# A fixed TensorE order for the experts' stage, weight buffers cut from one tile by hand, and the last weights in three transfers

## The chip, the cores and the metric

The kernel runs on one core of one Trainium2 chip, and reads all its weights from device memory. The metric is the device time of one execution in microseconds (us), where less is better. Engines are named as the profile names them: PE is TensorE, DVE is VectorE, ACT is ScalarE, POOL is GpSimd, and SP is the queue from which nearly all weight transfers are issued.

## The reference

Two blocks are computed in float32 for 256 tokens of width 1024:

```
def first_block(x, ...):
    for l in range(2):
        x = layer_norm(ALPHA * x + swiglu_half(x, w1[l], w3[l], w2[l]), ...)   # d_ff 2816
        h = x @ w_in[l]
        ...      # spatial gating, gated delta rule, gated linear attention
        x = layer_norm(ALPHA * x + mix @ w_out[l], ...)
        x = layer_norm(ALPHA * x + swiglu_half(x, ...), ...)

def second_block(x, c, ...):
    ...          # modulation from c, two kinds of attention, residual
    h2 = rms_norm_2(x, norm2_g) * (1.0 + scale2) + shift2
    return x + gate2 * moe_ffn(h2, ...)

def moe_ffn(h, ...):                     # 32 experts, the 4 best of each token
    ...
    gu = xe @ w_gate_up[e] + b_gate_up[e]                 # 1024 -> 2048
    g = min(gu[:, :1024], 7); u = clip(gu[:, 1024:], -7, 7)
    act = (u + 1) * (g * sigmoid(1.702 * g))
    y = act @ w_down[e] + b_down[e]                       # 1024 -> 1024
    # y times the token's gate, summed over its four experts
```

Each expert has 12 MiB of weights, so the 32 experts read 402.65 MB.

## The kernel before

**Dense stages** (the first block and the second block's attention). Weights come in transfers of 1 MB (0.5 MB for the first four) into `raw`, a pool of two buffers of 2 MB. `raw_half` (L142) gives out the two halves of one buffer, one after the other, and takes the next buffer when both are gone; `piece` (L151, transfer on L154) fills a half. `split` (L186, L187) makes of each 128x1024 part a rounded `wh` on ACT and a remainder `wl` on DVE, which TensorE multiplies (L161 and others). A framework's scheduler sets the order in which instructions stand on each engine and puts in the waits; a new buffer of a pool waits until every reader of the old one is done. On ACT and DVE the splits stand in one row with the work on the products (`tmp` L295, `ab` L297, `sl` L299, `gT` L302).

**Experts' stage.** Every expert gets 64 slots for tokens, and a part after it, skipped here, repeats experts that have more. `moe_order` (L1140) lists the 192 pieces of 2 MB: four of `gate_up` for an expert, then two of `down` for the expert before it. `moe_slots` (L1165) names nine buffers in turn, two of them from `raw`, and `prefetch` (L1173, transfer on L1177) issues a piece as soon as the buffer's last reader is done. Per expert, TensorE does this:
- `gate_up` (L1220): four pieces of 16 records each (L1230: every float32 matmul shows as two) into a two-bank PSUM tile `gu`, then the bias as eight records of a 32-row product (L1234).
- DVE and ACT make `act` of `gu` (L1237 to L1241).
- `down` (L1244), for the expert before: four transposes of `act` into the first bank of a tile `td` (L1249), a copy to SBUF on ACT (`aT`, L1251), two pieces of 16 records into the second bank (L1256), the bias (L1259), the product with `g2` on DVE, which gives `y` (L1261); two transposes of the gates (L1264), their copy `GT` on ACT (L1266), and `y` back to the tokens' places in eight records (L1270) that add up in four further banks over all experts.
- Every fourth expert `tokens` (L1196) gathers the tokens of the next four, with 32 records (L1207) and two copies on ACT (L1208).

All PSUM tiles come from pools in turn, and the scheduler decides what stands between what; it puts transposes and gathers between pieces. `moe` (L1345) has the loop, and `leave` (L1282 to L1285) copies the sums out and writes the result.

Of the kernel before, what the change touches and what calls it, by code (L numbers as in the profile page):

```python
# [16 lines left out]
P = 128  # L17
D = 1024
KD = D // P
T = 256  # L20
# [17 lines left out]
class Kernel:  # L38
    def __init__(self, ctx, tc, a, out):
# [4 lines left out]
        self.raw = pool("raw", 2)  # L44
# [8 lines left out]
        self.uid, self.spare = 0, None  # L53
# [1086 lines left out]
    def moe_order(self):  # L1140

        for e in range(33):
            if e < 32:
                yield from (self.gu_piece(e, i) for i in range(4))
            if e:
                yield from (self.dn_piece(e - 1, q) for q in range(2))
# [18 lines left out]
    def moe_slots(self):  # L1165

        self.spare = None
        while True:
            for name in ("rawE", "xp", "slotp", "raw", "slotp", "raw", "raw2", "slotp", "raw2"):
                tag = {"xp": "xT", "slotp": "slot"}.get(name, name)  # L1170
                yield getattr(self, name).tile([P, 4096], F32, tag=tag, name=self.n("rawm"))

    def prefetch(self, n, queue=None):  # L1173
        for _ in range(n):
            src, r = next(self.order), next(self.slots)
            v = r.rearrange("p (k f) -> p k f", k=src.shape[1])
            (queue or self.nc.sync).dma_start(v, src)  # L1177
            self.ready.append(v)

    def moe_piece(self, src):  # L1180
        if src is not None:
            r = self.raw.tile([P, 4096], F32, tag="raw", name=self.n("rawm"))
            v = r.rearrange("p (k f) -> p k f", k=src.shape[1])
# [12 lines left out]
    def tokens(self, XT, lo, hi):  # L1196
# [3 lines left out]
        for k0 in range(0, KD, 4):  # L1200
            w = self.wide()
            wv = w.rearrange("p a (b c) -> p (a b) c", b=2)[:, :, lo:hi]
            for k in range(4):
                i, j = divmod(k0 + k, 2)
                for t in range(2):
                    h = self.h2[t].rearrange("p (i m j) -> p i j m", i=4, j=2)[:, i, j]
                    nc.tensor.matmul(wv[:, k], h, at[:, t, lo:hi], start=(t == 0), stop=(t == 1))  # L1207
            nc.scalar.activation(XT[:, k0 : k0 + 4, lo:hi], wv, AF.Copy)  # L1208
# [11 lines left out]
    def gate_up(self, src, sel, XT):  # L1220
        nc = self.nc
        gu = self.wide()
        for i in range(4):
            r = self.moe_piece(src(i))
            for j in range(2):
                k = 2 * i + j
                for b in range(2):
                    for c in range(2):
                        f0 = b * 1024 + c * 512
                        nc.tensor.matmul(gu[c * 64 : c * 64 + 64, b], XT[:, k], r[:, j, f0 : f0 + 512], start=(k == 0), stop=False)  # L1230
        for b in range(2):
            for c in range(2):
                j = slice(32 * (2 * b + c), 32 * (2 * b + c) + 32)
                nc.tensor.matmul(gu[c * 64 : c * 64 + 64, b], sel[j], self.bgu[j], start=False, stop=True)  # L1234
        g, u, s = self.mg, self.mu.pop(0), self.ms
        self.mu.append(u)
        nc.vector.tensor_scalar(g, gu[:, 0], 7.0, None, op0=OP.min)  # L1237
        nc.vector.tensor_scalar(u, gu[:, 1], 7.0, -7.0, op0=OP.min, op1=OP.max)
        nc.scalar.activation(s, g, AF.Sigmoid, scale=1.702)  # L1239
        nc.vector.scalar_tensor_tensor(u, u, 1.0, g, op0=OP.add, op1=OP.mult)  # L1240
        nc.vector.tensor_tensor(u, u, s, op=OP.mult)  # L1241
        return u

    def down(self, src, sel, act, G, acc, first, last):  # L1244
        nc = self.nc
        td = self.wide()
        av = act.rearrange("p (m s) -> p s m", s=4)
        for s in range(4):
            nc.tensor.transpose(td[:, 0, s * P : (s + 1) * P], av[:, s], self.ident)  # L1249
        aT = self.aT  # L1250
        nc.scalar.activation(aT, td[:, 0].rearrange("p (s c i) -> p s c i", s=4, c=2), AF.Copy)  # L1251
        for q in range(2):
            r = self.moe_piece(src(q))
            for s in range(4):
                for c in range(2):
                    nc.tensor.matmul(td[c * 64 : c * 64 + 64, 1], aT[:, s, q], r[:, s, c * 512 : (c + 1) * 512],  # L1256
                                     start=(q == 0 and s == 0), stop=False)
        for c in range(2):
            nc.tensor.matmul(td[c * 64 : c * 64 + 64, 1], sel[0:32], self.bd[:, c * 512 : (c + 1) * 512], start=False, stop=True)  # L1259
        y = self.ms  # L1260
        nc.vector.tensor_tensor(y, td[:, 1], self.g2, op=OP.mult)  # L1261
        tg = self.wide()
        for t in range(2):
            nc.tensor.transpose(tg[:, 0, t * P : (t + 1) * P], G[t].rearrange("p d s -> p (d s)"), self.ident)  # L1264
        GT = self.GT
        nc.scalar.activation(GT, tg[:, 0, :T], AF.Copy)  # L1266
        for t in range(2):
            for c in range(2):
                r = slice(c * 64, c * 64 + 64)
                nc.tensor.matmul(acc[t][c], GT[r, t * P : (t + 1) * P], y[r, :], start=first, stop=first or last, skip_group_check=True)  # L1270
# [16 lines left out]
    def overflow(self, acc):  # L1287
# [3 lines left out]
        with tc.If(most > 64):  # L1291
            with tc.For_i(0, 32, 1) as e:
                have = nc.values_load(self.cnt[0:1, bass.ds(e, 1)], min_val=0, max_val=T)

                def part(r):
# [8 lines left out]
                    self.tokens(XT, 0, 64)  # L1304
                    G = self.gated(oh, [gt[:, t] for t in range(2)], 1)
                    gu = lambda i: self.gu_piece(e, i)
                    dn = lambda q: self.dn_piece(e, q)
                    self.down(dn, sel, self.gate_up(gu, sel, XT[:, :, :64]), [g[:, 0] for g in G], acc, False, True)
# [378 lines left out]
```

## Time and profile before

| | us |
|---|---|
| median of three runs | 2303.39 (2297.19 to 2309.14) |
| profiled execution, own time | 2300.92 |
| its span | 2299.1 |
| PE busy in the span | 2167.1 (94%) |
| start of the experts' pieces on PE | 1352.57 |
| start of the last eight records (L1270) | 2289.36 |

The span is the profiled execution from the first to the last instruction; its own time is 1.82 us longer. PEclk is the TensorE clock granted, as a share of full speed.

### The profile page before, as it was taken

Reading aid. Unit: us, or ns where it says so; the run is one execution under the profiler, and the core shown is the slowest. Engines: PE = TensorE matmul, PEld = TensorE weight load, DVE = VectorE, ACT = ScalarE, POOL = GpSimd, SP = SyncE. Lnnn points to the kernel's source line nnn. Section 1 sums busy time; section 2 is a strip of 40 time slices with the busy share of each in tenths; the row PEclk is TensorE's granted clock in tenths of the full one; section 3 lists DMA queues with packets and bytes.
Section 4 is the critical chain, followed back from the end, with each engine's and each line's share of the span. In section 5 each row is a group of like instructions: output and inputs, shape, how many; then the busy total and the mean of one; then the engine's idle time right before and its main releaser. Section 6 shows DMA issues by size and latency. Waiting matters only on the chain. (4 is left out here: it accounts for less than half of the span.)

```text
span 2299.1 us, 27689 instructions
## 1 busy us (share of the span) xinstructions
PE 2167.1 (94%) x11342; PEld 1375.1 (60%) x11343; DVE 1063.3 (46%) x1656; ACT 752.8 (33%) x1110; POOL 187.9 (8%) x214
## 2 busy tenths in 40 slices
PE   7999998999899999899989789999999999999998
PEld 6888877888788887778867553333332333333332
DVE  5866866966776686676676721111111111101011
ACT  4555843555455584245547520000000000000000
POOL 1001222001100122200020300000000000000000
PEclk9999999999999999999999879999999999999999
DMA  8854432956775443266554379999999999999994
GB/s 255 311 184 155 142 105 86 326 188 200 266 256 183 151 138 116 73 218 217 177 210 153 123 295 420 412 425 425 427 427 428 428 427 427 428 428 428 427 427 182
DMA packets 193156, 637.63 MB, mean 277 GB/s; under 512 B 24128, under 2 KB 131616, under 8 KB 168448
## 3 DMA queue, kind: packets, MB, share of 16 engines
q1 hardware_dynamic: 175920, 622.95, 69.6%
q0 software_dynamic: 3760, 11.28, 1.7%
q10 hardware_dynamic: 13344, 1.57, 0.4%
q8 instruction: 91, 1.49, 0.3%
q14 instruction: 41, 0.34, 0.0%
HBM read 633.91 MB, written 1.86 MB: 277 GB/s over the span
## 5 line engine op out<-in xcount | busy, mean ns | idle before, releaser
L187 DVE TENSOR_TENSOR wl<-raw,wh 128x1024 fp32r<-128x1024 f32 x332 | 407.6, 1233 | 201.8 <-ACT wh L186 201.5
L186 ACT ACTIVATE wh<-raw 128x1024 fp32r<-128x1024 f32 (+1 forms) x350 | 366.5, 1051 | 375.7 <-PE w L161 136.1
L161 PE MATMUL w<-xT,wh 128*128 128x512 f32 x1344 | 478.1, 397 | 6.8 <-DVE ab L297 6.8
L1230 PE MATMUL w<-rawm,XT 128*64 128x512 f32 x2048 | 463.3, 599 | 2.1 <-ACT wh L1266 2.1
L162 PE MATMUL w<-xT,wl 128*128 128x256 f32 x1344 | 379.6, 282 | 0.0
L1230 PEld LDWEIGHTS w<-rawm,XT 128*64 128x64 f32 x2048 | 141.4, 137 | 279.0 <-issue 270.4
L1237 DVE TENSOR_SCALAR wl<-w 128x512 f32<-128x512 f32 x32 | 22.1, 692 | 608.9 <-PE w L1234 608.9
L161 PEld LDWEIGHTS w<-xT,wh 128*128 128x128 f32 x1344 | 254.9, 190 | 67.6 <-DVE ab L297 7.5
L162 PEld LDWEIGHTS w<-xT,wl 128*128 128x128 f32 x1344 | 254.1, 189 | 1.5
L1256 PE MATMUL w<-rawm,wh 128*64 128x512 f32 x1024 | 232.7, 598 | 3.7 <-ACT wh L1251 3.7
L309 PE MATMUL m<-wh,gT 128*128 128x512 f32 x592 | 190.9, 393 | 0.0
L1251 ACT ACTIVATE wh<-w 128x512 f32<-128x512 f32 x32 | 19.1, 597 | 449.2 <-PE w L1249 444.7
L1256 PEld LDWEIGHTS w<-rawm,wh 128*64 128x64 f32 x1024 | 68.2, 136 | 144.4 <-issue 139.7
L309 PEld LDWEIGHTS m<-wh,gT 128*128 128x128 f32 x592 | 111.2, 188 | 26.9 <-issue 1.7
L309 PE MATMUL m<-wl,gT 128*128 128x512 f32 x296 | 116.3, 393 | 0.0
L1261 DVE TENSOR_TENSOR wl<-w,wl 128x512 f32<-128x512 f32 x32 | 22.1, 692 | 191.5 <-PE w L1259 191.5
L386 PE MATMUL w<-wh,xT 128*128 128x512 f32 (+1 forms) x224 | 89.3, 399 | 6.0 <-DVE xT L236 6.0
L384 PE MATMUL w<-wh,xT 128*128 128x512 f32 (+1 forms) x224 | 90.7, 407 | 2.5 <-ACT pre L711 2.0
L385 PE MATMUL w<-wl,xT 128*128 128x512 f32 (+1 forms) x224 | 88.7, 396 | 4.5 <-DVE wl L187 4.5
L1216 POOL TENSOR_TENSOR G<-wl 128x256 f32<-128x256 f32 x32 | 19.7, 647 | 841.7 <-PE w L1264 825.7
L1239 ACT ACTIVATE wl<-wl 128x512 f32<-128x512 f32 x32 | 20.1, 629 | 207.5 <-DVE wl L1237 207.5
L1270 PE MATMUL m<-wl,wh 64*128 64x512 f32 x256 | 63.6, 613 | 18.6 <-DVE wl L1261 18.6
(469 smaller groups left out, 2740.6 us busy)
## 6 DMA issues: line engine op xcount, KB each, us to landing
rawm<-in_w_gate_up_dram SPq DMA_DIRECT2D x126, 2048.0 KB
raw<-in_ffn_w_dram SPq DMA_DIRECT2D x130, 1024.0 KB
rawm<-in_w_down_dram SPq DMA_DIRECT2D x64, 2048.0 KB
raw<-in_w_in_dram SPq DMA_DIRECT2D x36, 1024.0 KB
adaw<-in_w_ada_dram SPq DMA_DIRECT2D x48, 512.0 KB
raw<-in_w_out_dram SPq DMA_DIRECT2D x12, 1024.0 KB
rawm<-in_w_gate_up_dram POOLq DMA_DIRECT2D x2, 2048.0 KB, 8.5
raw<-in_w_in_dram SPq DMA_DIRECT2D x4, 544.0 KB
```

Of the source, the lines that this page charges most:

```text
L161: nc.tensor.matmul(w[:, ab], h[:, k], self.xT[:, k], start=(k == 0), stop=False)
L162: nc.tensor.matmul(w[:, ab, :T], l[:, k], self.xT[:, k, :T], start=False, stop=(k == KD - 1))
L186: nc.scalar.activation(h, v, AF.Copy)
L187: (low or nc.vector).tensor_tensor(l, v, h.bitcast(F32), op=OP.subtract)
L309: mm = lambda g, w, start, stop: nc.tensor.matmul(acc[t][q], g, w[:, 0, q * 512 : (q + 1) * 512], start=start, stop=stop, skip_group_check ...
L384: self.nc.tensor.matmul(w[:, t, :n], xh, h, start=(k == 0), stop=False)
L385: self.nc.tensor.matmul(w[:, t, :n], xh, l, start=False, stop=False)
L386: self.nc.tensor.matmul(w[:, t, :n], xl, h, start=False, stop=(k == KD - 1))
L1230: nc.tensor.matmul(gu[c * 64 : c * 64 + 64, b], XT[:, k], r[:, j, f0 : f0 + 512], start=(k == 0), stop=False)
L1237: nc.vector.tensor_scalar(g, gu[:, 0], 7.0, None, op0=OP.min)
L1256: nc.tensor.matmul(td[c * 64 : c * 64 + 64, 1], aT[:, s, q], r[:, s, c * 512 : (c + 1) * 512], start=(q == 0 and s == 0), stop=False)
L1270: nc.tensor.matmul(acc[t][c], GT[r, t * P : (t + 1) * P], y[r, :], start=first, stop=first or last, skip_group_check=True)
```

## The change

Four things change.
1. `raw` is one tile of four parts of 8 KB per partition, handed out by a counter (`raw_half`), and two neighbouring parts are one of the nine buffers of the experts (`raw_pair`). So the framework sees which part an instruction reads, and a load waits for the readers of its own part alone.
2. The experts' stage has two PSUM tiles, `gu` and `td`, for its whole length, and TensorE's instructions stand there in the order in which the code writes them (`manual_schedule`). The other engines are still ordered by the scheduler. The bias of each product comes first, and the gathered tokens go into `gu` and `td`.
3. The last expert's second `down` piece goes out as three transfers, of 1 MB, 0.5 MB and 0.5 MB, where other pieces are one.
4. `mu`, the buffer of `act`, is one where it was two in turn, and the sigmoid is issued before `u` is clipped.

```diff
-        self.raw = pool("raw", 2)
+        self.raw = pool("raw").tile([P, 4, 2048], F32, name="raw")
...
-        if self.spare is None:
-            x = self.raw.tile([P, 2, 2048], F32, tag="raw", name=self.n("raw"))
-            self.spare = x[:, 1]
-            return x[:, 0]
-        x, self.spare = self.spare, None
-        return x
+        return self.raw[:, next(self.turn) % 4]
+
+    def raw_pair(self):
+
+        i = 2 * (next(self.turn) % 2)
+        return self.raw[:, i : i + 2].rearrange("p k f -> p (k f)")
...
-                yield from (self.dn_piece(e - 1, q) for q in range(2))
+                yield from ((self.dn_piece(e - 1, q), (0, 2, 3, 4) if e == 32 and q else (0, 4)) for q in range(2))
...
-            (queue or self.nc.sync).dma_start(v, src)
+            for k0, k1 in itertools.pairwise(cuts):
+                (queue or self.nc.sync).dma_start(v[:, k0:k1], src[:, k0:k1])
...
+    def act_T(self, td):
+
+        av = self.mu.rearrange("p (m s) -> p s m", s=4)
         for s in range(4):
-            nc.tensor.transpose(td[:, 0, s * P : (s + 1) * P], av[:, s], self.ident)
...
+            self.nc.tensor.transpose(td[:, s * P : (s + 1) * P], av[:, s], self.ident)
+        self.nc.scalar.activation(self.aT, td.rearrange("p (s c i) -> p s c i", s=4, c=2), AF.Copy)
...
     def moe(self):
-        nc, a = self.nc, self.a
-        prev = G = None
+        with self.tc.manual_schedule(engines={mybir.EngineType.PE}):
+            acc = self.experts()
+        self.leave(acc)
+        self.overflow(acc)
+
+    def experts(self):
...
+        gu, td = self.wide(), self.wide()
+        XT, oh = self.gather(of(self.place, 0), 4)
+        for k0, w in ((0, gu), (4, td)):
+            self.tokens(XT, 0, 64, k0, w)
+        for e in range(34):
             if e < 32:
...
+                up = self.gate_up(gu, listed, sel(e), XT[:, :, (e % 4) * 64 : (e % 4) * 64 + 64])
+                next(up)
             if e == 0:
-                self.tokens(XT, 64, 256)
+                self.gates()
             if e == 1:
                 acc = [[self.bank() for _ in range(2)] for _ in range(2)]
...
+            if e > 1:
+                self.back(acc, e == 2, e == 33)
+            if e < 32:
+                next(up)
+            if 0 < e < 33:
+                self.gates_T(td[:, 0], [g[:, (e - 1) % 4] for g in G])
+            if e < 32:
+                drain(up)
...
+            if 0 < e < 33:
+                more = e % 4 == 3 and e < 31
+                dn = self.down(td[:, 1], listed, sel(e - 1))
...
+                for i, _ in enumerate(dn):
+                    if more and i in (1, 2):
+                        self.tokens(XT, 0, 256, 4 * i - 4, gu)
+            if e < 32:
+                self.act_T(td[:, 0])
+        return acc
```

Where the order moves can be seen at three places. The first is PE in the experts' stage before, from the `down` of one expert to the `gate_up` of the next (L1230, L1256: `gate_up` and `down` pieces; L1249: transposes of `act`; L1234, L1259: biases; L1264: transposes of the gates; L1270: back to the tokens):

```order
L1256 MATMUL w_13165<-rawm_13181,wh_11477 64x512 [waits DMAHW1_49]
L1256 MATMUL w_13165<-rawm_13181,wh_11477 64x512 x7
L1259 MATMUL w_13165<-wl_11479,eye_154 64x512 x2
L1270 MATMUL m_11744<-wl_11480,wh_11477 128x512 [waits DVE_49,Activation_49]
L1270 MATMUL m_11745<-wl_11480,wh_11477 128x512
L1270 MATMUL m_11746<-wl_11480,wh_11477 128x512
L1270 MATMUL m_11747<-wl_11480,wh_11477 128x512
L1230 MATMUL w_13208<-rawm_13209,XT_13094 64x512 [waits DMAHW2_49,PE_49]
L1230 MATMUL w_13208<-rawm_13209,XT_13094 64x512 x7
L1249 MATMUL w_13258<-ident,wh_11476 128x128 [waits PE_49]
L1249 MATMUL w_13258<-ident,wh_11476 128x128 x2
L1230 MATMUL w_13208<-rawm_13219,XT_13094 64x512 [waits DMAHW3_49]
```

After the change the same stretch is written on other lines (L1235, L1260: pieces; L1248: transposes of `act`; L1227, L1255: biases; L1270: transposes of the gates; L1279: back to the tokens; a wait is shown in square brackets):

```order
L1260 MATMUL w_11501<-rawm_12305,wh_11382 64x512 x7
L1248 MATMUL w_11501<-ident,wh_11381 128x128 [waits DVE_49]
L1248 MATMUL w_11501<-ident,wh_11381 128x128 x3
L1227 MATMUL w_11500<-wl_11383,eye_155 64x512 x4
L1235 MATMUL w_11500<-rawm_12325,XT_12186 64x512 [waits DMAHW2_49]
L1235 MATMUL w_11500<-rawm_12325,XT_12186 64x512 x7
L1279 MATMUL m_11623<-wl_11385,wh_11382 128x512
L1279 MATMUL m_11624<-wl_11385,wh_11382 128x512
L1279 MATMUL m_11625<-wl_11385,wh_11382 128x512
L1279 MATMUL m_11626<-wl_11385,wh_11382 128x512
L1235 MATMUL w_11500<-rawm_12339,XT_12186 64x512 [waits DMAHW3_49]
L1235 MATMUL w_11500<-rawm_12339,XT_12186 64x512 x7
```

The rows for the way back stood behind the bias of `down`; they now stand behind the first piece of the next expert but one, and the transposes of `act` stand in one place, directly behind the pieces of `down`, with a wait for DVE.

The second place is SP at the program's start before (`raw`: 1 MB of weights; `adaw`: modulation weights; `ln_g`, `ln_b`: a norm's two vectors, spread over the partitions):

```order
L154 DMA raw_192<-in_ffn_w_dram 128x8x128 x2
L154 DMA raw_195<-in_ffn_w_dram 128x8x128 x2
L767 DMA adaw_457<-in_w_ada_dram 128x1024
L767 DMA adaw_459<-in_w_ada_dram 128x1024
L191 DMA ln_g<-in_ln_g_dram 128x1024 [waits DMAHW0_49]
L191 DMA ln_b<-in_ln_b_dram 128x1024 [waits DMAHW1_49]
L154 DMA raw_343<-in_ffn_w_dram 128x8x256 [waits DMAHW2_49,DMAHW3_49,DVE_49,Activation_49]
L154 DMA raw_343<-in_ffn_w_dram 128x8x256
L154 DMA raw_485<-in_ffn_w_dram 128x2x1024 [waits DMAHW5_49,DMAHW4_49,DVE_49]
L154 DMA raw_485<-in_ffn_w_dram 128x8x256
```

After the change:

```order
L154 DMA raw<-in_ffn_w_dram 128x8x128 x4
L767 DMA adaw_455<-in_w_ada_dram 128x1024
L767 DMA adaw_457<-in_w_ada_dram 128x1024
L154 DMA raw<-in_ffn_w_dram 128x8x256 [waits DMAHW0_49,DMAHW2_49,DVE_49,Activation_49]
L154 DMA raw<-in_ffn_w_dram 128x8x256 [waits DMAHW1_49,DMAHW3_49,DVE_49,Activation_49]
L154 DMA raw<-in_ffn_w_dram 128x2x1024 [waits DMAHW4_49,DVE_49]
L154 DMA raw<-in_ffn_w_dram 128x8x256 [waits DMAHW5_49,DVE_49]
L191 DMA ln_g<-in_ln_g_dram 128x1024
```

The four loads of `raw` now stand ahead of `ln_g` and `ln_b`, and each has a wait of its own; before, the first of a pair waited for both old halves.

The third place is ACT at the same point before (`wh`: the split of a 128x1024 part, L186, the first two shown of the 0.5 MB loads; `tmp`: the first product leaves its PSUM tile, L295):

```order
L186 ACTIVATE wh_290<-raw_195 128x1024 [waits DMAHW4_49]
L186 ACTIVATE wh_310<-raw_195 128x1024 [waits DMAHW5_49]
L186 ACTIVATE wh_348<-raw_343 128x1024 [waits DVE_49,DMAHW2_49,PE_49,Activation_49]
L295 ACTIVATE tmp_279<-w_206 128x512 [waits PE_49]
L299 ACT_TABLE_LOAD
L299 ACTIVATE sl_283<-ab_281 128x256 [waits DVE_49]
```

After the change:

```order
L186 ACTIVATE wh_289<-raw 128x1024 [waits DMAHW4_49]
L186 ACTIVATE wh_309<-raw 128x1024 [waits DMAHW5_49]
L186 ACTIVATE wh_346<-raw 128x1024 [waits DVE_49,DMAHW0_49,PE_49,Activation_49]
L186 ACTIVATE wh_366<-raw 128x1024 [waits DVE_49,DMAHW1_49,PE_49,Activation_49]
L295 ACTIVATE tmp_278<-w_205 128x512 [waits PE_49]
L186 ACTIVATE wh_397<-raw 128x1024 [waits DVE_49,PE_49]
L299 ACT_TABLE_LOAD
L299 ACTIVATE sl_282<-ab_280 128x256 [waits DVE_49]
```

Behind the 0.5 MB parts, `tmp` now stands behind two splits, which read two different loads (each has a transfer of its own among its waits), where it stood behind one.

## Rows read from the trace of the kernel before

**Rows 1.** Windows of 57.5 us: busy time of each engine, PEclk, DMA share, GB/s

```profile
1782.50:1840.00 57.50, 56.97 (x264) 21.92 (x262) 6.50 (x10) 5.27 (x8) 1.68 (x3) 1.00 1.01 428
2242.50:2300.00 57.50, 45.69 (x207) 14.44 (x202) 6.29 (x10) 4.17 (x8) 0.00 (x0) 0.97 0.42 176
```

**Rows 2.** The chain that ended last, 1345 to 2299: shares, then start, us, line

```profile
by line: PE w L1230 48.0%; PE w L1256 24.0%; PE w L1207 6.9%; PE m L1270 6.6%; PE w L1259 3.4%; PE w L1234 3.4%; PE w L1249 2.7%; DVE wl L1261 1.5%; PE w L1264 1.3%; issue 0.5%; ACT wh L1266 0.5%; ACT wh L1251 0.3%; DVE xn L1284 0.1%; DVE w
...
1701.86 10.45 PE w L1230 x48
...
1818.66 10.45 PE w L1230 x48
```

**Rows 3.** The transfer queue's waits, 1200 to 2299: us in total, times, longest

```profile
SPq L1177 <- PE w L1230: 508.7, 106, 17.5
```

**Rows 4.** PE's timeline in the experts' stage: start, us, line, count, [idle <-releaser]

```profile
1814.50 4.16 PE L1207 MATMUL w<-wl,wh 128*128 128x256 f32 x18
...
1841.86 1.07 PE L1259 MATMUL w<-wl,eye 32*64 32x512 f32 x4
1843.82 1.99 PE L1270 MATMUL m<-wl,wh 64*128 64x512 f32 x8 [0.89 <-DVE wl L1261]
1845.74 3.65 PE L1230 MATMUL w<-rawm,XT 128*64 128x512 f32 x16
1849.32 0.63 PE L1249 MATMUL w<-ident,wh 128*128 128x128 f32 x3
1849.88 3.65 PE L1230 MATMUL w<-rawm,XT 128*64 128x512 f32 x16
1853.47 0.39 PE L1249 MATMUL w<-ident,wh 128*128 128x128 f32 x1
1853.78 7.09 PE L1230 MATMUL w<-rawm,XT 128*64 128x512 f32 x32
1860.80 1.09 PE L1234 MATMUL w<-wl,eye 32*64 32x512 f32 x8
1861.82 3.65 PE L1256 MATMUL w<-rawm,wh 128*64 128x512 f32 x16
1865.40 0.44 PE L1264 MATMUL w<-ident,G 128*128 128x128 f32 x2
...
1869.35 1.07 PE L1259 MATMUL w<-wl,eye 32*64 32x512 f32 x4
```

**Rows 5.** PE's timeline at the stage's start

```profile
1352.57 16.52 PE L1230 MATMUL w<-rawm,XT 128*64 128x512 f32 x64
...
1370.04 5.48 PE L1207 MATMUL w<-wl,wh 128*128 128x192 f32 x32
1375.45 13.95 PE L1230 MATMUL w<-rawm,XT 128*64 128x512 f32 x64
```

**Rows 6.** PE's timeline at the end

```profile
2289.36 1.99 PE L1270 MATMUL m<-wl,wh 64*128 64x512 f32 x8 [0.94 <-DVE wl L1261]
```

**Rows 7.** A window of 1 us near the last bytes

```profile
2266.00:2267.00 1.00, 1.00 (x10) 0.20 (x8) 0.00 (x0) 0.00 (x0) 0.00 (x0) 1.00 0.12 49
```

**Rows 8.** ACT's timeline in the first feed-forward part

```profile
32.82 1.06 ACT L186 ACTIVATE wh<-raw 128x1024 fp32r<-128x1024 f32 x1 [13.07 <-DMA raw<-in_ffn_w_dram]
33.78 0.58 ACT L295 ACTIVATE tmp<-w 128x512 f32<-128x512 f32 x1
```

**Rows 9.** The transfer queue's timeline at the start

```profile
20.00 9.50 SPq L154 DMA_DIRECT2D raw<-in_ffn_w_dram  x4
```

**Rows 10.** Windows of two stretches in the dense stages

```profile
30.00:36.00 6.00, 2.78 (x17) 2.20 (x16) 1.83 (x2) 3.06 (x4) 0.00 (x0) 1.00 1.07 373
36.00:42.00 6.00, 6.00 (x26) 5.16 (x26) 5.26 (x8) 5.23 (x9) 0.00 (x0) 0.72 0.59 210
580.00:590.00 10.00, 5.81 (x17) 3.97 (x16) 7.70 (x11) 3.68 (x5) 4.53 (x3) 0.66 0.71 217
```

**Rows 11.** ACT's timeline in the second layer

```profile
578.12 1.06 ACT L186 ACTIVATE wh<-raw 128x1024 fp32r<-128x1024 f32 x1 [4.10 <-DMA raw<-in_ffn_w_dram]
```

More of the change, by code (lines that the diff above doesn't have):

```diff
@@ L1143, in moe_order @@
             if e < 32:
-                yield from (self.gu_piece(e, i) for i in range(4))
+                yield from ((self.gu_piece(e, i), (0, 2)) for i in range(4))
             if e:
-                yield from (self.dn_piece(e - 1, q) for q in range(2))
+                yield from ((self.dn_piece(e - 1, q), (0, 2, 3, 4) if e == 32 and q else (0, 4)) for q in range(2))
     def gu_piece(self, e, i):
@@ L1181, in moe_piece @@
         if src is not None:
-            r = self.raw.tile([P, 4096], F32, tag="raw", name=self.n("rawm"))
-            v = r.rearrange("p (k f) -> p k f", k=src.shape[1])
+            v = self.raw_pair().rearrange("p (k f) -> p k f", k=src.shape[1])
             self.nc.sync.dma_start(v, src)
@@ L1218, in gated, with gate_up @@
         return G
-    def gate_up(self, src, sel, XT):
+    def gate_up(self, gu, src, sel, XT):
         nc = self.nc
-        gu = self.wide()
+        for b in range(2):
+            for c in range(2):
+                j = slice(32 * (2 * b + c), 32 * (2 * b + c) + 32)
+                nc.tensor.matmul(gu[c * 64 : c * 64 + 64, b], sel[j], self.bgu[j], start=True, stop=False)
         for i in range(4):
@@ L1255, in down, with gates_T, back @@
                 for c in range(2):
[L1256 to L1262, printed above, removed]
+                    nc.tensor.matmul(td[c * 64 : c * 64 + 64], self.aT[:, s, q], r[:, s, c * 512 : (c + 1) * 512],
+                                     start=False, stop=(q == 1 and s == 3))
+                if s % 2:
+                    yield
+        nc.vector.tensor_tensor(self.ms, td, self.g2, op=OP.mult)
+    def gates_T(self, tg, G):
+        nc = self.nc
         for t in range(2):
-            nc.tensor.transpose(tg[:, 0, t * P : (t + 1) * P], G[t].rearrange("p d s -> p (d s)"), self.ident)
-        GT = self.GT
-        nc.scalar.activation(GT, tg[:, 0, :T], AF.Copy)
+            nc.tensor.transpose(tg[:, t * P : (t + 1) * P], G[t].rearrange("p d s -> p (d s)"), self.ident)
+        nc.scalar.activation(self.GT, tg[:, :T], AF.Copy)
+    def back(self, acc, first, last):
+        nc = self.nc
         for t in range(2):
@@ L1269, in down @@
                 r = slice(c * 64, c * 64 + 64)
-                nc.tensor.matmul(acc[t][c], GT[r, t * P : (t + 1) * P], y[r, :], start=first, stop=first or last, skip_group_check=True)
+                nc.tensor.matmul(acc[t][c], self.GT[r, t * P : (t + 1) * P], self.ms[r, :], start=first, stop=first or last, skip_group_check=True)
         if first:
@@ L1322, in moe_tiles @@
         self.h2 = H[:2]
-        self.mu = [H[2][:, 0:512], H[2][:, 512:]]
+        self.mu = H[2][:, 0:512]
         self.aT = H[3][:, 0:512].rearrange("p (s c i) -> p s c i", s=4, c=2)
```

87 lines of the change are left out of this document (39 added, 48 removed).

## The prediction

> **What bounds the kernel now.** I read the busy shares by windows first, then the chain that ended last, then who waits for whom on the transfer queue, and then TensorE's timeline.
>
> In the middle of the experts' stage PE is busy 56.97 of 57.5 us, and DMA is at 1.01 of its time with 428 GB/s [rows 1]: both are full. The chain says which ends last. From the stage's start it consists of PE lines, 48.0% and 24.0% for the two kinds of pieces, and no DMA stands in it [rows 2]. The transfer queue agrees: a load waits for a buffer that PE still reads (508.7 us in 106 waits for `gate_up` pieces alone) [rows 3]. So TensorE sets the end, and the transfers follow close behind. A piece of 2.097 MB takes 4.90 us at 428 GB/s, four experts 24 x 4.90 = 117.6 us, and PE takes 1818.66 - 1701.86 = 116.80 us for four [rows 2]. That PE is the faster and yet the bound is no contradiction: nine buffers give transfers a lead of up to 9 x 4.90 = 44 us, which is used up slowly. The last bytes land in the window 2266 to 2267, where DMA is at 0.12 [rows 7]; the last records start at 2289.36 [rows 6].
>
> **PE per expert, before.** Starts of consecutive rows give the cost of each group, gaps included [rows 4]. From bias to bias an expert takes 1869.35 - 1841.86 = 27.49 us. In it: bias of `down` with the wait behind it 1843.82 - 1841.86 = 1.96, of which about 1.00 is the bias and 0.96 the wait for `y` (the profile marks 0.89 as idle on DVE L1261); the way back 1.92; a piece of 16 records that is followed by others 3.58; the transposes 0.56 + 0.31 when cut in two; two pieces in one run 7.02; the bias of `gate_up` 1.02; a `down` piece with the gates' transposes behind it 1869.35 - 1865.40 = 3.95 less 3.58, so 0.37. The expert with a gather takes 116.80 - 3 x 27.49 = 34.33.
>
> **PE per expert, after.** The new order has the same records and fewer changes of group. Bias of `gate_up` 1.02, piece 3.58, way back 1.92, piece 3.58, gates' transposes 0.37, two pieces 7.02, bias of `down` 1.00, two pieces 7.02, and all four transposes in one place, 0.68 (the three and the one were 0.87 together, so one change of group, about 0.19, is saved).
>
> What becomes of the wait for `y` is the question. The way back no longer has it: it stands a piece later, and the 1.02 + 3.58 us in between cover 0.96. But the transposes of `act` write the first bank of `td`, whose second bank `y` is read from, and the order shows a wait for DVE there. Both banks are one tile. Directly behind the last `down` piece, that wait ends when `y` has been made. So I take the same 0.96 us, now in front of the transposes, with the bias of the next `gate_up` and its five pieces queued behind it. From below it is 0 (if the wait for DVE were for `act` alone, which is made while `down`'s pieces run); from above I have no row over 0.96 for this pair. The value is the upper one, as the operation and what it waits for are the same.
>
> Sum: 1.02 + 3.58 + 1.92 + 3.58 + 0.37 + 7.02 + 1.00 + 7.02 + 0.96 + 0.68 = 27.15 us, 0.34 below before. The gather: 18 of its 32 records take 4.16 us [rows 4], so 16 take about 3.65 and 32 take 7.30; they stand around halves of a `down` piece, which is one more change of group (0.2): +7.5 us, so 34.65, which is 0.3 above before.
>
> Over the stage: the first piece starts at 1352.57, where the clock is still at half: those 64 records take 16.52 us and the next 64 take 13.95 [rows 5], so 2.5 more. The first expert's own gather is 5.4 us, 1375.45 - 1370.04 [rows 5], and 0.5 for a wait on its copy; 0.5 more for the gates' work, now between two pieces. 32 x 27.15 + 7 x 7.5 + 5.4 + 0.5 + 0.5 + 2.5 = 930.2, so the last records end at 2282.8. Before, they end at 2289.36 + 1.99 = 2291.35 [rows 6]. The stage gains **8.5 us**. The early experts, whose transposes stood unhidden before, give most of it.
>
> **Transfers.** PE's four experts now take 3 x 27.15 + 34.65 = 116.1 us against 117.6 for their transfers: PE eats 1.5 us of the lead in a period, some 12 us of 44 in eight. I take no wait. The end of the last records, 2282.8, stays 16 us behind the last bytes, so cutting the last piece is worth nothing: its first use is 3.58 + 0.96 + 1.92 = 6.5 us ahead of the end, at 2276, after its landing. Two more issues on the queue have nothing behind them but the output, 16 us later.
>
> **The parts of `raw` in the dense stages.** PE stalls where the order of loads is changed. At the start, ACT waits 13.07 us for a part of `raw`, until 32.82 [rows 8], and its first copy from PSUM stands behind that. PE is busy only 2.78 of the 6 us from 30 to 36, and its clock is 0.72 in the next six [rows 10]: 3.2 + 6 x 0.28 = 4.9 us. The load is one of four that SP issues from 20.00 on [rows 9], when both old halves are free. After the change the first waits for its half alone and stands ahead of `ln_g` and `ln_b`; it can be issued some 5 us earlier. Against that, ACT's copy now stands behind two splits, of two loads. Bounds 0 and -4.9; I take -4, as the second load would have to be 10 us slower to matter. The modulation weights and the norms' vectors move back in the queue by a few transfers; no engine waits for them here, so 0.
>
> At 578.12 ACT has waited 4.10 us for `raw` [rows 11], and from 580 to 590 PE is busy 5.81 us at a clock of 0.66 [rows 10]: 4.2 idle and 5.81 x 0.34 = 2.0 of clock, 6.2 us. Here each load can go out one split (1 to 2 us) earlier. Bounds 0 and -6.2; I take -2, in proportion to 1.5 of 4.1. Other stages have no such stall that I can tie to `raw`: 0, with +-2 for rows that the scheduler has moved by one or two places.
>
> Sum: -8.5 - 4 - 2 = -14.5. The profiled execution's own time 2300.92 becomes 2286.4. The runs' median lies 2.47 above it, so I predict **2288.9 us**, 0.6% below 2303.39. A difference of 0.5% (11.5 us, below 2291.9) is about what can be told from no change here.
>
> **A rule of the Trainium skill.** Over the window with PE busy 56.97 of 57.5 us and one 0.89 us wait per expert, the granted clock was 1.00 [rows 1, 4]. "TensorE: Matmul & The Clock Gate" (HAM oscillation — how this bites in real kernels) says that a TensorE that idles briefly and often between groups of matmuls can swing between its two clock levels and lose throughput. The trace does not agree for a wait of this size; after the 3.2 us stall at the start it does. By the rule the moved wait could cost clock, which is the third rival.
>
> **Rivals.**
> 1. The wait for `y` is hidden after all. For it: `act` is ready long before. Then 32 x 0.96 = 31 us would go, but PE would be ready at 2252 and must wait for the last bytes at 2267, a quarter piece (0.9), `y` (0.96) and the way back (1.92): 2271, a gain of 20 us, and with the dense 6 us 2300.92 - 26 + 2.47 = 2277. Against it: the wait for DVE in the order. Chance 0.13.
> 2. The dense stages gain nothing: ACT is held by the second load as long as by the first before, or the transfers share the time. Then 2300.92 - 8.5 + 2.47 = 2294.9, within 0.5%. For it: DMA is at 1.07 from 30 to 36 [rows 10], so an earlier issue may only lengthen the flight. Chance 0.27.
> 3. Slower: the wait in front of the transposes is longer than before, since `y` is queued on DVE or TensorE loses clock in it. All of TensorE stands behind it. The stage's gain is gone from 8.5 / 32 = 0.27 us more per expert. At 1 us more (a clock of half over the next 2 us would do it) the stage is 32 - 8.5 = 23.5 us longer: 2300.92 + 23.5 - 6 + 2.47 = 2320.9. Against it: no row shows a wait for `y` over 0.96. Chance 0.07.
> 4. PE's switches cost the same wherever they are, and nothing moves: 2303. Chance 0.03.
>
> The forecast has 0.5, with its own range 2284 to 2294. Below 2291.9 lie 0.45 of that and rival 1: 0.58 faster; 0.05 of it and rivals 2 and 4: 0.35 same; rival 3: 0.07 slower. The range leaves out the ends of rivals 1 and 3: 2275 to 2299.
>
> **What would show it.** On PE's timeline of after: plain experts 27.15 us apart, an idle of about 0.9 in front of L1248 put down to DVE L1264, none in front of L1279. At 30 to 36 PE busy for nearly all six, and ACT's wait for `raw` ending well before 30. DMA at 1.0 until about 2266, and the last records (L1279) ending near 2283 less what the dense stages gave. The prediction is wrong if the wait at L1248 is gone or longer, if PE waits for DMA in the stage, or if the dense stages end later.

## The result, and the profile after

The changed kernel takes 2277.22 us (median of four runs, 2272.54 to 2278.03) against 2305.85 us (four runs) of the kernel before: a ratio of 0.9877, 95% interval 0.9846 to 0.9909. It is faster by 28.6 us, 1.2%. Forecast were 2288.9 us and a gain of 14.5 us. The time lies in the range, 2275 to 2299, but 11.7 us below the forecast and below the forecast's own range of 2284 to 2294.

The profiled executions differ by 2299.1 - 2275.1 = 24.0 us of span. (The other 4.6 us stand in neither trace: the profiled execution before lay 4.9 us below the median of the four runs, the one after 0.3 us below its own.) Two points on TensorE divide the 24.0 us: the first gather of tokens and the last records. After the change, on PE's timeline (start, us, line, count, idle before and what ended it):

```profile
1332.07 7.09 PE L1208 MATMUL w<-wl,wh 128*128 128x64 f32 x32 [1.37 <-DVE wl L1196]
1339.09 1.98 PE L1227 MATMUL w<-wl,eye 32*64 32x512 f32 x8
```

```profile
2265.37 1.99 PE L1279 MATMUL m<-wl,wh 64*128 64x512 f32 x8 [0.85 <-DVE wl L1264]
```

The gather started at 1345.55 before and starts at 1332.07 now: **the dense stages gave 13.5 us**. From the gather to the end of the last records it was 2291.35 - 1345.55 = 945.80 us and is 2267.36 - 1332.07 = 935.29: **the experts' stage gave 10.5 us**. The rest of the span behind is 7.7 us in both.

A plain expert on PE's timeline of after, which answers to [rows 4]:

```profile
1846.85 3.60 PE L1260 MATMUL w<-rawm,wh 128*64 128x512 f32 x16
1851.25 0.75 PE L1248 MATMUL w<-ident,wh 128*128 128x128 f32 x4 [0.79 <-DVE wl L1264]
1851.93 1.09 PE L1227 MATMUL w<-wl,eye 32*64 32x512 f32 x8
1852.94 3.65 PE L1235 MATMUL w<-rawm,XT 128*64 128x512 f32 x16
1856.53 1.99 PE L1279 MATMUL m<-wl,wh 64*128 64x512 f32 x8
...
1878.31 0.75 PE L1248 MATMUL w<-ident,wh 128*128 128x128 f32 x4 [0.80 <-DVE wl L1264]
```

From transposes to transposes it is 1878.31 - 1851.25 = 27.06 us. The idle of 0.79 us in front of L1248 is the wait for `y`, and L1279, the way back, waits for nothing. The list of PE's waits over the whole stage (us in total, times, longest) says the same for all experts, and no wait for DMA stands behind these two lines:

```profile
PE w L1248 <- DVE wl L1264: 24.6, 31, 0.8
PE m L1279 <- DVE wl L1264: 0.8, 1, 0.8
```

The dense stages, in windows (busy time of PE, PEld, DVE, ACT, POOL, then PEclk, DMA share, GB/s); first two windows of the kernel before beside those of [rows 10], then windows after the change:

```profile
285.00:305.00 20.00, 17.83 (x72) 13.50 (x73) 13.17 (x19) 11.39 (x20) 3.50 (x6) 0.83 0.63 180
985.00:1000.00 15.00, 11.41 (x51) 9.62 (x51) 7.54 (x12) 5.78 (x9) 0.00 (x0) 0.77 0.62 223
```

```profile
30.00:36.00 6.00, 3.71 (x22) 2.99 (x21) 4.14 (x4) 4.06 (x5) 0.00 (x0) 1.00 0.94 334
285.00:305.00 20.00, 19.13 (x100) 14.21 (x97) 14.81 (x22) 15.07 (x24) 5.93 (x10) 1.00 0.54 165
985.00:1000.00 15.00, 15.00 (x80) 12.80 (x79) 12.18 (x16) 9.53 (x15) 0.00 (x0) 1.00 0.93 339
```

At 285 and at 985 PE was idle for 2.2 and 3.6 us with a clock of 0.83 and 0.77, and is busy at 1.00 now (0.9 us idle, and none). I had named neither stretch. At 30 to 36, where I had expected most, PE is still busy only 3.71 of 6 us.

### The profile page after: what moved, and what is told of

Same layout as the page of the kernel before. It is cut to its first block, busy times and chain, and to the rows that moved or that the text cites. A ratio compares the mean times of both kernels' runs of the same rounds, so it can differ in the third digit from the quotient of the medians.

```text
span 2275.1 us, 27676 instructions
## 1 busy us (share of the span) xinstructions
PE 2152.0 (95%) x11342; PEld 1368.0 (60%) x11343; DVE 1060.4 (47%) x1656; ACT 754.3 (33%) x1110; POOL 186.7 (8%) x214
## 5 line engine op out<-in xcount | busy, mean ns | idle before, releaser
L186 ACT ACTIVATE wh<-raw 128x1024 fp32r<-128x1024 f32 (+1 forms) x350 | 366.3, 1051 | 367.3 <-PE w L161 129.0
L1235 PE MATMUL w<-rawm,XT 128*64 128x512 f32 x1696 | 383.6, 599 | 0.0
L1235 PEld LDWEIGHTS w<-rawm,XT 128*64 128x64 f32 x1696 | 115.6, 137 | 246.6 <-issue 246.5
L1260 PE MATMUL w<-rawm,wh 128*64 128x512 f32 x704 | 159.0, 596 | 0.0
L1264 DVE TENSOR_TENSOR wl<-w,wl 128x512 f32<-128x512 f32 x32 | 22.1, 692 | 225.7 <-PE w L1260 225.7
L1271 ACT ACTIVATE wh<-w 128x256 f32<-128x256 f32 x32 | 12.3, 383 | 306.3 <-PE w L1270 306.3
L1260 PEld LDWEIGHTS w<-rawm,wh 128*64 128x64 f32 x704 | 47.9, 137 | 103.8 <-issue 103.8
L1249 ACT ACTIVATE wh<-w 128x512 f32<-128x512 f32 x32 | 19.1, 597 | 214.4 <-PE w L1248 214.4
```

Of the source, the lines that this page charges most:

```text
L186: nc.scalar.activation(h, v, AF.Copy)
L1260: nc.tensor.matmul(td[c * 64 : c * 64 + 64], self.aT[:, s, q], r[:, s, c * 512 : (c + 1) * 512], start=False, stop=(q == 1 and s == 3))
```

## The experiments

The ratio compares a run with the kernel before, run beside it on the same chip. "Gather" is the start of the first gather in the profiled execution (1345.55 in the one of the kernel before), "stage" the time from there to the end of the last records (945.80 before).

| run | ratio, 95% interval | gather | stage |
|---|---|---|---|
| the changed kernel again | 0.9892 (0.9866 to 0.9919) | 1332.63 | 935.54 |
| parts of `raw` alone | 0.9933 (0.9913 to 0.9953) | 1335.98 | 945.81 |
| order of PE alone | 0.9950 (0.9932 to 0.9968) | 1346.89 | 934.81 |
| last piece whole | 0.9896 (0.9871 to 0.9921) | 1333.97 | 935.55 |
| early transposes | 0.9866 (0.9838 to 0.9894) | 1335.18 | 929.93 |
| early transposes, last piece whole | 0.9872 (0.9842 to 0.9901) | 1335.85 | 930.38 |
| way back at once | 0.9858 (0.9830 to 0.9886) | 1335.72 | 933.26 |
| early transposes, router's split later, short tail | 0.9868 (0.9844 to 0.9892) | 1332.80 | 928.39 |
| router's split later, before | 0.9979 (0.9962 to 0.9997) | 1343.98 | 944.80 |
| small transfers on POOL, before | 1.0006 (0.9992 to 1.0020) | 1347.36 | 945.69 |
| three parts | 0.9873 (0.9844 to 0.9901) | 1337.57 | 935.04 |

**The two halves of the change.** The kernel before with the parts of `raw` alone:

```diff
-        self.raw = pool("raw", 2)
+        self.raw = pool("raw").tile([P, 4, 2048], F32, name="raw")
...
+        return self.raw[:, next(self.turn) % 4]
```

> The kernel before with the parts of raw alone; the experts' stage is in its old order. Theory A (the dense gain belongs to the parts of raw): the first gather of the experts' stage starts near 1332 instead of 1345.6, about 13.5 us earlier, the stage itself keeps its 945.8 us from the first gather to the end of the last records, and the time falls by 13.5 us. Theory B (the dense gain is luck of one execution, or belongs to the other edits): the gather starts near 1340 to 1346 and the time falls by less than 6 us.

And the changed kernel with the pool of pairs put back:

```diff
-        self.raw = pool("raw").tile([P, 4, 2048], F32, name="raw")
+        self.raw = pool("raw", 2)
...
-        return self.raw[:, next(self.turn) % 4]
```

> The changed kernel with raw as a pool of two buffers again; TensorE's fixed order, the biases first and the last piece in three remain. Theory A: the first gather starts near 1345 as before the change, a plain expert takes 27.05 us, the stage takes 935 us, and the time falls by 10.5 us. Theory B: the dense stages are as short as after the change (gather near 1332), and the time falls by 20 us or more.

Measured medians are 2289.5 and 2291.4 us against 2303.5: -14.0 and -12.1. The parts alone leave the stage at 945.81 and move the gather by 9.6 us, less than the 13.5 of theory A; the order alone leaves the gather (+1.3) and shortens the stage by 11.0. The effects add up, and theory B fails in both runs. "Order alone" still has the third and the fourth point of the change; the third is tested below, the fourth (one `mu`, the sigmoid's place) in no run. The changed kernel once more:

> The changed kernel once more, beside the two others of this job. Expected: 0.988 of the time before; the first gather of the experts' stage within 4 us of 1332 (dense stages of the same code have differed by 2 to 4 us from execution to execution), the stage within 1 us of 935.3.

It agrees: 12.9 and 10.3 us. Where in the dense stages the parts gain can be read by following the same PE instructions through the timelines. The table has how much earlier (-) or later (+) than in the kernel before they start, in us; the instruction is named by its start before.

| run | 262 | 303 | 385 | 579 | 590 | 846 | 960 | 1000 | gather |
|---|---|---|---|---|---|---|---|---|---|
| changed | -2.6 | -6.7 | -4.9 | -5.8 | -2.9 | -3.9 | -7.7 | -13.0 | -13.5 |
| changed, again | +1.1 | -3.7 | -1.0 | -1.7 | +1.3 | 0.0 | -5.4 | -10.7 | -12.9 |
| parts alone | +0.5 | -4.0 | -1.3 | -2.0 | +0.9 | -0.1 | -4.5 | -9.4 | -9.6 |
| last piece whole | +0.2 | -3.7 | -4.8 | -5.0 | -2.2 | -2.5 | -6.1 | -11.3 | -11.6 |
| order alone | +1.6 | +1.4 | +4.5 | +3.9 | +3.4 | +3.2 | +2.8 | +3.6 | +1.3 |

With the parts, 4 to 5 us are gained from 262 to 303 in every execution (0.2 without them), and up to 2.7 of that is given back by 385 (the order alone loses 3.1 there); 2.8 to 3.0 are lost from 579 to 590 (0.5 are gained without them); 3.6 to 5.4 are gained from 846 to 960, where the second layer repeats the stretch of 262 to 385; and 4.9 to 5.3 from 960 to 1000. Up to 262, the first feed-forward part, there is no gain that repeats.

What is lost from 579 to 590 stands in PE's waits from 560 to 600, before and after, and on ACT's timeline after:

```profile
PE m L309 <- ACT gT L302: 4.2, 1, 4.2
```

```profile
PE m L309 <- ACT gT L302: 7.3, 2, 5.7
575.26 2.94 ACT L186 ACTIVATE wh<-raw 128x1024 fp32r<-128x1024 f32 x3
578.11 0.57 ACT L295 ACTIVATE tmp<-w 128x512 f32<-128x512 f32 x1
```

After the change three splits stand in one row on ACT ahead of a product's copy (L295), from which `gT` is made, where one split stood ahead of it before, at 578.12 [rows 11]; PE waits longer for `gT`.

**The start.** ACT's timeline of the changed kernel, which answers to [rows 8]:

```profile
28.86 1.06 ACT L186 ACTIVATE wh<-raw 128x1024 fp32r<-128x1024 f32 x1 [9.20 <-DMA raw<-in_ffn_w_dram]
31.91 1.06 ACT L186 ACTIVATE wh<-raw 128x1024 fp32r<-128x1024 f32 x1 [1.99 <-DMA raw<-in_ffn_w_dram]
32.87 0.58 ACT L295 ACTIVATE tmp<-w 128x512 f32<-128x512 f32 x1
```

The four loads go out from 15.19 on, 4.8 us earlier, as forecast, and ACT has the first 4 us earlier. But the copy of the first product (L295) stands behind two splits now, and starts at 32.87, where it started at 33.78. In the second execution of the same kernel PE was busy for less of this stretch than before the change:

```profile
30.00:36.00 6.00, 1.67 (x11) 1.22 (x9) 3.13 (x4) 3.18 (x5) 0.00 (x0) 0.88 1.01 358
```

**985 to 1000.** Before, ACT waits there for the router's weights, a small transfer; on ACT's timelines of before and after:

```profile
992.12 0.42 ACT L868 ACTIVATE wrs<-wr 128x256 fp32r<-128x256 f32 x1 [6.18 <-DMA wr<-in_w_router_dram]
```

```profile
980.41 0.42 ACT L868 ACTIVATE wrs<-wr 128x256 fp32r<-128x256 f32 x1 [2.85 <-DMA wr<-in_w_router_dram]
```

It lands 13.7 us after its issue before (14.9 with the order alone), and 10.1 us after it with the change (9.8 with the parts alone). On POOL's queue it stands behind two transfers of 512 KB, which land late themselves (before, then after; the last number is the median time from issue to landing in us):

```profile
row<-mods POOLq DMA_DIRECT2D x2, 512.0 KB, 13.1
```

```profile
row<-mods POOLq DMA_DIRECT2D x2, 512.0 KB, 8.1
```

To see whether this wait is the stall, the split of these weights was put behind the product's copy, with `raw` as before:

```diff
-        nc.scalar.activation(w[:, :, 0], wr, AF.Copy)
...
+        def split():
+            nc.scalar.activation(w[:, :, 0], wr, AF.Copy)
...
-                hook={3: lambda: self.second_consts(bp), 5: lambda: next(gain1)})
+                hook={3: lambda: self.second_consts(bp), 5: lambda: next(gain1), 6: route_split})
```

> The kernel before, with the split of the router's weights (L868 on ACT) placed behind the first product's copy from PSUM instead of ahead of it. Theory A (the stall at 985 to 1000 is ACT waiting for that small transfer, whose landing takes 13.7 us with the pool of pairs and 10 us with the parts): TensorE doesn't stall there, its clock stays at 1.0, and the time falls by 3 to 5 us with no edit of raw. Theory B (the stall is due to raw itself): no change.

```profile
985.00:1000.00 15.00, 14.20 (x90) 12.56 (x89) 8.18 (x12) 6.98 (x10) 0.00 (x0) 1.00 0.53 198
```

PE is busy 14.20 of 15 us at full clock. Its instructions start 3.5 us later than before at 960 (the first 960 us are the same code) and 1.7 us earlier at 1000: 5.2 us gained in place, as much as the parts give. The median is 5.0 us lower (0.7 to 8.8 by the interval). Theory A holds.

**285 to 305.** In the gated delta rule, ACT issues two small transfers to device memory and then four back, which wait for the first two. ACT's row behind them, before and after:

```profile
294.81 0.38 ACT L626 ACTIVATE gqk<-m 128x256 f32<-128x256 f32 x1 [4.79 <-issue]
```

```profile
290.48 0.38 ACT L626 ACTIVATE gqk<-m 128x256 f32<-128x256 f32 x1 [2.23 <-issue]
```

ACT is held 4.79 us (2.23 after), and PE waits 1.76 us for its next row, after which the clock falls to half. Before, the hold is longer because the first two transfers move later. ACT issues both within 0.4 us, from 287.73 on before and from 285.76 on after. In the next 3.4 us (287.8 to 291.2 before, 285.8 to 289.2 after) these queues move data (q1 is SP's, q10 ACT's; packets, MB, share of the 16 engines' time):

```profile
q1 hardware_dynamic: 418, 1.32, 103.3%
```

```profile
q10 hardware_dynamic: 1118, 0.32, 38.4%
q1 hardware_dynamic: 92, 0.31, 22.5%
```

Before, weight loads take all of that time and nothing of ACT's queue moves; its packets start at 291.24, when those of SP's queue end (291.55). There SP's queue has 2.10 MB under way, two loads of 1 MB, since a buffer of the pool comes free as a pair; with the parts it is one load of 1.05 MB, through at 286.73. The second layer shows the same at 860, and so do the traces of the order alone (two loads) and of the parts alone (one).

The kernel before with these transfers on POOL:

```diff
-            nc.scalar.dma_start(s2[m].rearrange("h (b j) i -> (h b) j i", j=16), QT[:, m])
+            nc.gpsimd.dma_start(s2[m].rearrange("h (b j) i -> (h b) j i", j=16), QT[:, m])
...
-                nc.scalar.dma_start(self.QTc[:, m, t], s2[m, ...])
+                nc.gpsimd.dma_start(self.QTc[:, m, t], s2[m, ...])
```

> The kernel before, with the six small transfers of the gated delta rule's triangular inverse (QT to device memory and back, L1527 and L1529) issued by POOL instead of ACT. Theory A (ACT is held some 5 us at 290 by the issue that waits for the first transfer's landing, and TensorE's stall and half clock at 293 to 303 follow from it): no stall at 293, the clock stays at 1.0 there, and the time falls by 3 us in each of the two layers, 6 us. Theory B (the stall has another cause, or the transfers are slower from POOL): no change, or slower.

```profile
285.00:305.00 20.00, 15.47 (x80) 11.52 (x79) 14.85 (x21) 12.53 (x21) 8.30 (x12) 0.99 0.42 132
305.00:390.00 85.00, 78.95 (x524) 65.16 (x524) 51.15 (x90) 25.37 (x37) 21.35 (x22) 0.90 0.26 87
```

```profile
303.63 0.46 PE L642 MATMUL m<-incl,gxe 128*128 128x128 f32 x2 [3.51 <-DVE gxe L638]
```

The stall at 293 is gone and the clock stays at 0.99 up to 305, so that stall did come from ACT's hold. But PE is idle for 4.5 of these 20 us, more than before (2.2): DVE waits for the way back in device memory in one piece of 4.4 us, where it was 3.2 in two, PE waits 3.51 us for DVE at 303.63, and the clock is 0.90 behind that. PE is 1.8 us later than before at 262 and 3.5 us later at 385. The time is unchanged, against theory A's 6 us: this run shows where the stall came from, but not what its removal is worth.

**How early a load goes out.**

```diff
-        return self.raw[:, next(self.turn) % 4]
+        return self.raw[:, next(self.turn) % 3]
```

> The changed kernel with three of the four parts of raw in use in the dense stages; each load still waits for its own part alone. Theory A (what counts is how early a load can be issued): with one part less the loads go out one split later, TensorE stalls for weights, and the dense stages are longer by 5 us or more (slower than the changed kernel). Theory B (what counts is the order in which the scheduler has put things, or luck): the dense stages stay within 3 us.

With three parts a load can stand in the code ahead of a split that still needs the part's old contents, so some dense products read other weights than they should, and the run settles nothing on how much an earlier load is worth. At the start the loads do go out later (21.82), but the gather starts at 1337.57, only 1.6 us behind the latest run with four parts (1335.98).

**The wait for `y`.** The changed kernel with the transposes between the two pieces:

```diff
+                    if i == 1 and e < 32:
+                        self.act_T(td[:, 0])
...
-                self.act_T(td[:, 0])
+                self.act_copy(td[:, 0])
```

> The changed kernel with the four transposes of act between the two pieces of down, so that no y stands ahead of them; their copy to SBUF stays behind the second piece. Theory A (the wait for y costs TensorE 0.88 us in each expert, and behind it lie transfers that can't go faster): the wait goes, a plain expert takes 26.4 us (one more change of group), TensorE catches up with the transfers towards the end of the stage and waits for DMA there; the last bytes still land near 2253, the last records end 4 to 6 us behind them, and the time falls by 8 to 11 us below the changed kernel. Theory B (TensorE alone bounds the stage): 32 times 0.65 to 0.88, so 21 to 28 us below the changed kernel. Theory C (the wait only moves to the next reader of y): no change.

```profile
PE w L1235 <- DMA rawm<-in_w_gate_up_dram: 9.7, 13, 1.3
PE w L1263 <- DMA rawm<-in_w_down_dram: 2.9, 8, 0.6
PE m L1282 <- DVE wl L1267: 1.6, 2, 0.9
...
PE w L1235 <- DMA raw<-in_w_gate_up_dram: 1.3, 2, 0.9
PE w L1263 <- DMA raw<-in_w_down_dram: 1.0, 3, 0.6
```

```profile
2207.48 3.65 PE L1235 MATMUL w<-rawm,XT 128*64 128x512 f32 x16 [1.25 <-DMA rawm<-in_w_gate_up_dram]
...
2237.05 3.65 PE L1235 MATMUL w<-rawm,XT 128*64 128x512 f32 x16 [1.25 <-DMA rawm<-in_w_gate_up_dram]
...
2246.84 3.65 PE L1263 MATMUL w<-rawm,wh 128*64 128x512 f32 x16 [0.56 <-DMA rawm<-in_w_down_dram]
...
2255.18 7.09 PE L1263 MATMUL w<-rawm,wh 128*64 128x512 f32 x32
2263.12 1.99 PE L1282 MATMUL m<-wl,wh 64*128 64x512 f32 x8 [0.85 <-DVE wl L1267]
```

The 31 waits for `y` are two, and PE now waits for DMA, 14.9 us in 26 waits, as it does in no row of this stage before: from one expert's row to the next's it is 2237.05 - 2207.48 = 29.57 us, which is the pace of six pieces. An expert earlier in the stage, which waits for nothing, takes 26.35 us:

```profile
1832.83 1.07 PE L1258 MATMUL w<-wl,eye 32*64 32x512 f32 x4
...
1859.18 1.07 PE L1258 MATMUL w<-wl,eye 32*64 32x512 f32 x4
```

That is 0.71 us less than 27.06, or 22.7 us over 32 experts, of which the stage gets 935.3 - 929.9 = 5.4. Theory B fails, and the size in theory A was too high: the last bytes land at 2256 (the gather is 3.1 us later than in the changed kernel), when TensorE has only begun with the last two pieces, and the last records end 9 us behind them, not 4 to 6. The time is 0.9866 of before, against 0.9877 and 0.9892 in the two jobs of the changed kernel.

```diff
-            if e > 1:
-                self.back(acc, e == 2, e == 33)
...
+            if 0 < e < 33:
+                self.back(acc, e == 1, e == 32)
```

> As the run with early transposes, with the way back put directly behind the bias and pieces of its own down, so that it waits for y again. Theory A (one wait of 0.9 us for y per expert costs the same wherever it stands): a plain expert takes 27.1 to 27.3 us, an idle of 0.8 to 0.9 us in front of the way back, and the time is that of the changed kernel within 3 us (2 to 5 us above the run with early transposes, which the transfers bound). Theory B (where the wait stands matters): a plain expert takes over 27.5 us.

```profile
1849.47 0.75 PE L1248 MATMUL w<-ident,wh 128*128 128x128 f32 x4
...
1854.60 1.99 PE L1282 MATMUL m<-wl,wh 64*128 64x512 f32 x8 [0.79 <-DVE wl L1267]
...
1876.53 0.75 PE L1248 MATMUL w<-ident,wh 128*128 128x128 f32 x4
```

The wait is 0.79 us in front of the way back, and a plain expert takes 1876.53 - 1849.47 = 27.06 us, to the hundredth that of the changed kernel. So theory A holds for the plain expert: there the place of the wait doesn't matter. The stage is still 2.0 us shorter than in the changed kernel, as the experts with a gather take 34.32 us instead of 34.68. The time, 0.9858, is no longer than with early transposes, where theory A had 2 to 5 us more; the intervals overlap.

**The end.** The last piece as one transfer, in the changed kernel and with early transposes:

```diff
-(0, 2, 3, 4) if e == 32 and q else (0, 4)
+(0, 4)
```

> The changed kernel with the last piece as one transfer. Theory A (the last piece lands some 8 us before TensorE comes to it): no difference, within 1 us in the profile's stage length. Theory B (three transfers land the first part earlier and save a wait): 1 to 3 us slower.

> As the run before, with the last piece as one transfer. If the transfers bound the end there, TensorE must wait for the whole last piece: 1.5 to 3 us slower than with three transfers. If TensorE bounds the end, no difference.

The stages are 935.55 against 935.29, and 930.38 against 929.93: three transfers are worth nothing in the one and at most 0.5 us in the other. At last, the shortest tail:

```diff
+                dn = self.down((gu if e == 32 else td)[:, 1], listed, sel(e - 1))
...
+                    if i == 1 and e == 32:
+                        self.back(acc, False, False)
+                        self.gates_T(gu[:, 0], [g[:, 3] for g in G])
```

> Early transposes, the split of the router's weights one place later, and a shorter tail: the last expert's down goes into gu, which is free by then, and the way back of the expert before stands between its two pieces. Theory A (transfers bound the stage and TensorE's last three groups hang behind the last bytes): the tail's waits of 0.8 and 0.5 us go, some 1.5 us off the end; with 1 to 2 us at 985 it is 2 to 4 us faster than with early transposes alone, 0.985 of the time before. Theory B (the last bytes land later than I think): no gain at the end, and a wait for DMA in front of the last piece.

```profile
2243.08 3.65 PE L1266 MATMUL w<-rawm,wh 128*64 128x512 f32 x16 [0.56 <-DMA rawm<-in_w_down_dram]
...
2248.22 3.65 PE L1266 MATMUL w<-rawm,wh 128*64 128x512 f32 x16 [0.48 <-ACT wh L1255]
...
2254.69 3.65 PE L1266 MATMUL w<-rawm,wh 128*64 128x512 f32 x16 [0.53 <-ACT wh L1277]
2259.20 1.99 PE L1285 MATMUL m<-wl,wh 64*128 64x512 f32 x8 [0.85 <-DVE wl L1270]
```

The stage is 928.39 us, 1.5 less than with early transposes, and no wait for DMA stands in front of the last piece. That is theory A's size, but not its mechanism: from the last piece that waits for DMA to the end it is 2261.19 - 2243.08 = 18.1 us here and 2265.11 - 2246.84 = 18.3 us with early transposes, and waits of 0.48, 0.53 and 0.85 us stand in this tail where 0.80, 0.53 and 0.85 stood in the other. So 0.2 us of the 1.5 come from the tail, and the rest from the stretch ahead of it, in which PE keeps the pace of the transfers. The median, 2271.32 us, is the lowest of all, but its ratio (0.9868) is that of early transposes (0.9866), and its interval overlaps those of the other two variants and of the changed kernel in the same job (2277.16); between them the order is not settled.

## Why the prediction was right in the stage and wrong in the dense part

**The wait for `y`** was read rightly: it moved in front of the transposes (31 times, 24.6 us), and the way back has it once, at the end. It is 0.79 us rather than 0.89, as it is in front of the way back when pieces stand ahead of it there (the run "way back at once"); the plain expert takes 27.06 us rather than 27.15. In sum these waits grew, for before the stage had

```profile
PE m L1270 <- DVE wl L1261: 18.6, 21, 0.9
```

What the plain expert gained, 0.43 us, is the fewer changes of group that the sum counted, and 0.1 us of the wait.

**The stage** gained 10.5 us, not 8.5. The term that was off is 32 x 27.15: 0.09 us less in some 25 plain experts is 2.3 us. The rest of that sum holds: no wait for DMA, 34.68 us for an expert with a gather (34.65 forecast), nothing from cutting the last piece (tested), and 930.2 us were forecast from the first records behind the gather to the last where 2267.36 - 1339.09 = 928.3 came. What doesn't fit is the remark that the early experts "give most of it". By the sum's own terms 25 plain experts give 25 x 0.34 = 8.5 us and seven with a gather cost 7 x 0.32 = 2.2; measured, it is 25 x 0.43 = 10.8 less 7 x 0.36 = 2.5, so 8.2 of the 10.5 us, and about 2 are left for the early experts.

**The dense stages** gained 13.5 us (9.6 to 13.5 over the eight traces of kernels with the four parts, one of which also has the router's split later), not 6, and not where I put them. The step "I take -4" for the start failed: the load was issued 5 us earlier, as forecast, but ACT's copy stood behind a second load, the sentence that I had dismissed ("the second load would have to be 10 us slower to matter"). DMA was full already (share 1.07 [rows 10], 0.94 and 1.01 in two executions after), and ACT had the second load only at 31.91. That is the mechanism of the second rival, for this stretch. The step "I take -2" for 580 to 590 failed in sign: 2.8 to 3.0 us are lost, since the splits moved on ACT and PE's wait for `gT` grew by 3.1 us. And the step "Other stages have no such stall that I can tie to `raw`: 0" is where the gain was: two stretches in which TensorE waits for ACT, and ACT for a transfer that lands late (985 to 1000, shown by moving that wait), or for one whose issue holds its queue (262 to 303 and the same in the second layer, shown for the stall, not for its worth). I had looked for waits on `raw`, and those waits bear other names. Yet `raw` is behind the second: with the pool two loads of 1 MB go out at once, and ACT's small transfers move when both are through; with the parts they wait for one. For the router's weights the traces show only that all of POOL's queue lands earlier (8.1 against 13.1 us for the two transfers ahead); which of the moved loads does that is not shown.

**The first rival** would have come with the wait's removal: with early transposes TensorE does catch up with the transfers, as it said, but 5.4 us is what came of the 11.5 us more that it promised, since the last records end 9 us behind the last bytes and not 3.8. The third rival's clock loss at the moved wait didn't come: with 31 waits of 0.8 us the windows of the stage stay at a PEclk of 1.00. The rule of the Trainium skill on brief and frequent idles ("TensorE: Matmul & The Clock Gate", A second HAM failure mode: psum-queue depth-cycling, the section behind the one that I named) is not borne out for waits of this size. Behind the single wait of 1.76 us at 295 the clock did fall.

```profile
1782.50:1840.00 57.50, 55.91 (x260) 21.60 (x258) 6.27 (x10) 4.64 (x7) 2.51 (x4) 1.00 1.01 428
2185.00:2242.50 57.50, 55.91 (x262) 17.90 (x260) 6.73 (x10) 3.22 (x6) 0.00 (x0) 1.00 1.01 427
```

So the total fell in the range with a dense term that was right in sign, half its size, and wrong in place. That it fell in is luck: 2277 us is what the first rival gave, for whose sake the range went down to 2275, and its mechanism (no wait for `y`) did not come.

## What to carry to other kernels

When a load is let go earlier, follow every small transfer that shares the time with it, and who waits for it on an in-order engine: here 5 us hung on a transfer of the router's weights, and the list of waits on the loads that were moved didn't name it. Loads that go out in pairs keep a small transfer waiting for both (3.5 us here, 0.9 with one load). A wait that a reorder doesn't remove can cost the same in its new place, as 0.79 us did here; ask what the instruction behind it writes, and whether it is one tile with what is still being read. When an engine and the transfers run within 1.5% of one another, taking 2.6% off the engine's expert gives back a fraction of it (here 5.4 of 22.7 us), since the other takes over (14.9 us of waits for DMA).

## What was not expected of the hardware

A stall of 1.76 us on PE at 295 was followed by a stretch at the lower of its two clock levels, 1.2 GHz (a record of 128x512 took 0.63 us there and 0.40 at 2.4 GHz). A PEclk of 0.83 over the 20 us comes to 20 x 0.17 / 0.5 = 6.8 us at the lower level, or 3.4 us lost: twice what the stall itself lasted. The waits of 0.8 us once in 27 us in the experts' stage cost no clock (PEclk 1.00 in both windows above). Small transfers that ACT issued at 287.73 moved nothing for 3.5 us, until 2.1 MB of weight loads were through. And the same dense code began its stages 1 to 4 us earlier or later from execution to execution, as the table of starts shows between the kernels that differ in the experts' stage alone.
